# Differential attention units: GpSimd's product of the swapped rows with the sines is queued behind the last written addition of two softmax maps

## The chip, the core and the metric

The kernel runs on one core of one Trainium2 chip. The metric is the device time of one execution in microseconds (us); the time of a version is the median of its runs. Before the change it is 900.85 us, with three runs from 900.46 to 900.96.

The core has TensorE (PE in the profile, with its weight loads as PEld), VectorE (DVE), ScalarE (ACT), GpSimd (POOL) and SyncE (SP, which here only issues DMAs). Each works through a queue of its own in the order in which the program was laid out; between engines there are semaphores.

## The reference

A hybrid decoder block on x of 1024 rows by 1024 channels, float32. What matters here is the branch of differential attention, four heads with two maps each:

```python
h = rms_norm(x, g_pre)
qa, ka, va, fa, za, qb, kb, vb, zb, gates = split(h @ w_in)

def apply_rope(x, cos, sin):
    x1, x2 = split(x, 2, axis=-1)
    return concat([x1 * cos - x2 * sin, x2 * cos + x1 * sin])

qd = apply_rope(heads(qb), cos, sin)      # (heads, 2 maps, seq, 64)
kd = apply_rope(heads(kb), cos, sin)
p  = softmax(causal(qd @ kd.T / 8))       # both maps
pd = p[map 0] - lam * p[map 1]
yb = rms_norm(pd @ vd, g_subln) * (1 - lam_init)
```

Beside it runs an attention with forget gates (eight heads, no rope), both branches are gated, projected, merged and projected again, normalized, and added to x. None of that is touched.

## The kernel before

**Stages.** First the input is normalized and transposed (hT) and the values are projected (`v_block`). Then come eight attention units, u = 0 to 7: units 0 to 3 are the four differential heads, units 4 to 7 each hold two heads of the forgetting attention. Then come gates, branch projections and the output projection, which the change doesn't touch. float32 products are made from a rounded high part and a low part, so each projection has three matmuls for each of 8 slices of the contraction.

**A unit.** `unit_attn` makes four groups of two rows of 128 queries each. For a differential unit `row(i)` (lines 582 to 597) makes one row: `s_row` forms the scores of map 0 and of map 1 on PE (lines 492 and 493, tile S), DVE takes them out of PSUM with the mask and finds the extreme (line 495), ACT takes the exponential and the sum (line 501), DVE the reciprocal of both sums (line 591, tile l). GpSimd scales map 1 with its reciprocal and minus lambda (line 592), ACT scales map 0 (line 594), and GpSimd adds the two maps (line 595, the addition of the title). Later PE transposes the sum (line 522, tile pt), ACT and DVE split it in high and low part (lines 525, 526), and PE multiplies with the values (line 546). The width of row i is (i + 1) times 128, so in the profile the addition of row i of a unit is known by its shape: 128x128 is row 0, 128x1024 is row 7.

**Work laid between.** While unit u is attended, the projections of unit u + 1 are laid between its groups as fill tasks, in the order k first half (k0), q first half (q0), k second half (k1), q second half (q1), each half 512 columns; then the z projections of ZFILL. The loop at lines 708 to 723 writes the two rows of a group, the transposes and products of the group before, and then as many tasks as the weight of the groups done so far allows. By that count units 1 and 2 have k0 written behind row 1, q0 behind row 3, k1 and q1 behind row 5; unit 3, whose neighbour has four tasks and not six, has k0 behind row 1, q0 behind row 3, k1 behind row 5 and q1 behind row 7. The tasks of unit 0 are written before any row.

**Rope.** In a differential task the projected half lies in PSUM (tiles pk, pq of the pool pj, 2 buffers). `rope` (lines 359 to 371) copies it with ACT (line 362, raw), swaps blocks of 32 partitions with four small DMAs from SP's queue (line 366, raw to sw), multiplies with the cosines on DVE (line 368, rot), multiplies sw with the sines on GpSimd (line 369, the product of the title), and adds on DVE (line 370). `stack` then splits the result into high and low part (lines 378 and 379, tiles hi and lo) and sends both with four DMAs (lines 381 and 382) into TA, TB or KA, KB, from which the scores of the next unit are made.

**Buffers.** The tag "sw" has 2 buffers and serves sw and hi in turn; "raw" has 4 and serves raw, rot, lo and the staged z (line 432, tile sz, copied from PSUM at line 433). Taken in order, a rope with its stack takes three of "raw" and two of "sw". A staged z of units 1 and 2 follows twelve tiles of the four ropes, so the first z takes the buffer that lo of k1 had.

**Order on the engines.** The order in which each engine gets its instructions isn't the order of writing. The whole program is traced first, and a planner with its own estimate of durations (`schedule_with_timeline_sim=True`) orders each engine's queue by what it takes to be ready. `tc.issue_after(ins)` adds one constraint to that: what is traced in its block on the engine of `ins` comes behind `ins` in that engine's queue. It adds no instruction and no wait for the end of `ins`.

Of the kernel before, what the change touches and what calls it, by code (L numbers as in the profile page):

```python
# [12 lines left out]
ALU = mybir.AluOpType  # L13
# [32 lines left out]
def f32(ap):  # L46
    return ap.bitcast(F32)
# [3 lines left out]
def tile_hybrid_block(  # L51
# [18 lines left out]
    nc = tc.nc  # L70
# [54 lines left out]
    with ExitStack() as st:  # L125
# [152 lines left out]
        cosT, sinT, dmask = (big.tile([P, S], F32, tag="big", name=n) for n in ("cosT", "sinT", "dmask"))  # L278
# [27 lines left out]
                h_combinations(k)  # L306


    held = [None, None]

    def load_w(name, src, hi_act=False, lo_pool=False, pieces=None, behind=(None, None)):
        raw = wpool.tile([P, KT, P], F32, tag="wraw", name=f"raw_{name}")
# [17 lines left out]
    def project(ps, wt, c, ks=range(KT)):  # L330
        hi, lo = wt
        for k in ks:
            for a, h in ((hi, 0), (hi, 1), (lo, 0)):
                mm = nc.tensor.matmul(  # L334
                    ps, lhsT=a[:, k, :], rhs=hT[h][k // 4][c][:, k % 4, :],
                    start=(k == 0 and a is hi and h == 0), stop=(k == KT - 1 and a is lo))
        return mm.ins


    with ExitStack() as st:  # L340
# [9 lines left out]
        def unit_proj(u):  # L350

            diff = u < 4
            t = u if diff else u - 4
            qc, kc = (QB, KB_) if diff else (QA, KA_)
            T = {}
            for n in ("TA", "TB", "KA", "KB"):
                T[n] = qk.tile([P, S], F32R, tag=n, name=f"{n}{u}")

            def rope(ps, c, nm):
                sl = slice(c * CH, (c + 1) * CH)  # L360
                raw = stg.tile([P, CH], F32, tag="raw", name=f"raw{nm}", bufs=4)
                nc.scalar.copy(raw, ps)
                sw = stg.tile([P, CH], F32, tag="sw", name=f"sw{nm}")
                for b in range(4):
                    o = b ^ 1
                    nc.sync.dma_start(sw[b * 32:(b + 1) * 32, :], raw[o * 32:(o + 1) * 32, :])  # L366
                rot = stg.tile([P, CH], F32, tag="raw", name=f"rot{nm}", bufs=4)
                nc.vector.tensor_tensor(rot, ps, cosT[:, sl], op=ALU.mult)  # L368
                nc.gpsimd.tensor_tensor(sw, sw, sinT[:, sl], op=ALU.mult)
                nc.vector.tensor_tensor(rot, rot, sw, op=ALU.add)  # L370
                return rot

            def stack(A, B, src, sl, nm):

                if u > 0:
                    hi = stg.tile([P, CH], F32R, tag="sw", name=f"hi{nm}")
                    lo = stg.tile([P, CH], F32R, tag="raw", name=f"lo{nm}", bufs=4)
                    nc.scalar.copy(hi, src)
                    nc.vector.tensor_tensor(lo, src, hi, op=ALU.subtract)
                    for t, a, b in ((A, UPR, DNR), (B, DNR, UPR)):  # L380
                        nc.sync.dma_start(f32(t[a, sl]), f32(hi[a]))
                        nc.sync.dma_start(f32(t[b, sl]), f32(lo[a]))
                    return
                nc.scalar.copy(A[UPR, sl], src[UPR])
                nc.vector.tensor_tensor(A[DNR, sl], src[UPR], A[UPR, sl], op=ALU.subtract)
                nc.scalar.copy(B[DNR, sl], src[DNR])
                nc.vector.tensor_tensor(B[UPR, sl], src[DNR], B[DNR, sl], op=ALU.subtract)

            def q_chunk(wt, c):
                sl = slice(c * CH, (c + 1) * CH)  # L390
                ps = pj.tile([P, CH], F32, tag="pj", name=f"pq{u}_{c}")
                project(ps, wt, c)
                src = rope(ps, c, f"q{u}_{c}") if diff else ps
                stack(T["TA"], T["TB"], src, sl, f"q{u}_{c}")

            def k_chunk(wt, c):
                sl = slice(c * CH, (c + 1) * CH)
                ps = pj.tile([P, CH], F32, tag="pj", name=f"pk{u}_{c}")
                project(ps, wt, c)
                src = rope(ps, c, f"k{u}_{c}") if diff else ps  # L400
                stack(T["KA"], T["KB"], src, sl, f"k{u}_{c}")

            box = {}

            def mk(kind, c, c0):
                def run():
                    if kind not in box:
                        box[kind] = load_w(f"{kind}{u}", w_cols(c0))
                    (q_chunk if kind == "q" else k_chunk)(box[kind], c)
                return run  # L410

            tasks = [mk("k", 0, kc + t * P), mk("q", 0, qc + t * P),
                     mk("k", 1, kc + t * P), mk("q", 1, qc + t * P)]
            return T, tasks
# [146 lines left out]
        def unit_attn(u, T):  # L561
# [19 lines left out]
            if diff:  # L581
                def row(i, rows):
                    boff = S - (i + 1) * P
                    if "X" not in rows:
                        rows["X"] = [swapped(T, m, i // 2, f"d{u}") for m in range(2)]
                    le = small.tile([P, 2], F32, tag="l2", name=f"l{u}_{i}", bufs=4)
                    l1, l2 = le[:, 0:1], le[:, 1:2]
                    p1, _ = s_row(T, 0, i, rows["X"][0], dmask, boff, f"d{u}", l1)
                    p2, _ = s_row(T, 1, i, rows["X"][1], dmask, boff, f"d{u}", l2)
                    n = (i + 1) * P  # L590
                    nc.vector.reciprocal(le, le)
                    nc.gpsimd.tensor_scalar(
                        p2[:, 0:n], p2[:, 0:n], l2, nlam, op0=ALU.mult, op1=ALU.mult)
                    nc.scalar.activation(p1[:, 0:n], p1[:, 0:n], AF.Copy, scale=l1)
                    nc.gpsimd.tensor_tensor(
                        p1[:, 0:n], p1[:, 0:n], p2[:, 0:n], op=ALU.add)
                    rows[i] = p1

                def evac(g):
                    def run(yp):  # L600
                        ys = stg.tile([P, 2 * P], F32, tag="ys", name=f"ys{u}_{g}")
                        nc.scalar.copy(ys, yp)
                        nc.sync.dma_start(y_d[u][:, g * 2 * P:(g + 1) * 2 * P], ys)
                    return run

                for g in GORD[u]:
                    rows = {}
                    groups.append((
                        4 * g + 3,
                        [lambda i=i, rows=rows: row(i, rows) for i in (2 * g, 2 * g + 1)],  # L610
                        lambda g=g, rows=rows: av(rows, g, vt, 0, False, evac(g), f"d{u}_{g}", False)))
            else:
                ysb = {}

                def row(m, i, rows):
                    n = (i + 1) * P
                    diag = cb[m][:, n - P:n]
                    nc.gpsimd.tensor_tensor(diag, diag, trim, op=ALU.add)  # L618
                    if "X" not in rows:
                        rows["X"] = swapped(T, m, i // 2, f"f{u}")  # L620
                    p1, l1 = s_row(T, m, i, rows["X"], cb[m], 0, f"f{u}")
                    nc.vector.reciprocal(l1, l1)  # L622
                    held[1] = nc.gpsimd.tensor_scalar(  # L623
                        p1[:, 0:n], p1[:, 0:n], l1, 1.0, op0=ALU.mult, op1=ALU.mult).ins
                    rows[i] = p1

                def evac(m, g):
                    def run(yp):
                        if m == 0:
                            ysb[g] = stg.tile([P, 2 * P], F32, tag="ys", name=f"ys{u}_{g}")  # L630
                        tmp = stg.tile([P, 2 * P], F32, tag="yt", name=f"yt{u}_{m}_{g}", bufs=1)
                        nc.scalar.copy(tmp[64:128], yp[64:128])
                        nc.vector.tensor_tensor(
                            ysb[g][64 * m:64 * m + 64], yp[0:64], tmp[64:128], op=ALU.add)
                        if m == 1:
                            nc.sync.dma_start(y_d[u][:, g * 2 * P:(g + 1) * 2 * P], ysb[g])
                    return run

                for g in GORD[u]:
                    for m in range(2):  # L640
                        rows = {}
                        groups.append((
                            4 * g + 3,
                            [lambda m=m, i=i, rows=rows: row(m, i, rows) for i in (2 * g + 1, 2 * g)],
                            lambda m=m, g=g, rows=rows: av(
                                rows, g, vt, m * P, True, evac(m, g), f"f{u}_{m}_{g}",
                                u == 7 and g in FING)))
# [586 lines left out]
```

## Time and profile before

| | |
|---|---|
| median of 3 runs | 900.85 us (900.46 to 900.96) |
| the profiled execution's own time | 900.05 us |
| its span in the profile | 898.2 us |
| busy DVE, ACT, POOL over the span | 580.8, 429.5, 408.8 us |
| granted TensorE clock, mean | 0.998 |
| sine products (line 369) on POOL | 16, the median 1.29 us (four of them unit 0's) |
| additions of two maps (line 595) on POOL | 32, the median 1.43 us |

The times in the views run from the start of the span. The differential units lie at about 143 to 340 us, and the twelve sine products of units 1 to 3 between 144 and 282 us. In a timeline each row is one instruction or a few alike: start, duration, engine, line, operation, tile written and tiles read, shapes, the count, and in brackets the idle time of the engine just before with the event that ended it. A row of the waits names who waited for whom, with the total, the count and the longest. A row of the view by windows gives for each engine the busy time in that stretch.

### The profile page before, as it was taken

To read this page: it belongs to the slowest core of one execution; us is meant where nothing else is said; L and a number is where in the kernel's file an instruction comes from. 1 tells how busy PE (TensorE), PEld (TensorE's weight loads), DVE (VectorE), ACT (ScalarE), POOL (GpSimd) and SP (SyncE) were. 2 spreads that over 40 slices of the span, in tenths; PEclk is the share of its full clock that TensorE was granted. 3 is DMA by queue.
4 is the path that set the end of the run, shared out by engine and by line. 5 is a ranking of instruction groups with operands and counts; after the bars stand their busy time and mean duration, and the time that the engine had idled before them with its cause. 6 is when DMAs were issued, how large, how long until landed. Compare 5 with 4: busy or idle time off the path is not lost.

```text
span 898.2 us, 13825 instructions
## 1 busy us (share of the span) xinstructions
PE 882.4 (98%) x4612; PEld 746.5 (83%) x4612; DVE 580.8 (65%) x1124; ACT 429.5 (48%) x865; POOL 408.8 (46%) x400
## 2 busy tenths in 40 slices
PE   8999999999999999999999999999999999999997
PEld 6999987788888888888888888888888888888885
DVE  6766555868567644556547556626766896648797
ACT  7432225565766663464645646724443362314352
POOL 2234225636647544253444435516534323483963
PEclk9999999999999999999999999999999999999999
DMA  8576656656657754635636430397766598210495
GB/s 306 188 260 246 209 166 162 170 139 172 156 135 194 179 168 91 176 104 125 191 90 174 127 103 25 92 410 236 234 207 203 191 357 296 80 39 1 122 198 172
DMA packets 138186, 154.81 MB, mean 172 GB/s; under 512 B 12145, under 2 KB 98161, under 8 KB 137090
## 3 DMA queue, kind: packets, MB, share of 16 engines
q1 hardware_dynamic: 133744, 151.55, 55.8%
q0 software_dynamic: 4224, 2.10, 2.0%
q8 instruction: 37, 0.61, 0.3%
q14 instruction: 35, 0.29, 0.1%
q10 hardware_dynamic: 146, 0.27, 0.1%
HBM read 86.17 MB, written 38.34 MB: 139 GB/s over the span
## 4 chain that ended last, share of the span: by engine, by line
PE 75%; DMA 6%; DVE 5%; ACT 4%; SPq 4%; POOL 3%; issue 2%; POOLq 0%; DVEq 0%; ACTq 0%
PE x_g L831 15%; PE pb L991 10%; PE pv L214 10%; PE x_o L831 8%; PE pz L334 7%; PE pq L334 5%; PE pk L334 5%; PE ypf L546 3%; PE ptf L522 3%; SPq L366 2%; PE Sf L492 2%; PE Sf L493 2%; DMA swk<-rawk 1%; PE pg L334 1%; PE pgl L334 1%
## 5 line engine op out<-in xcount | busy, mean ns | idle before, releaser
L214 PE MATMUL pv<-wvhi,hT 128*128 128x264 f32 (+2 forms) x384 | 88.0, 323 | 0.3 <-ACT wvhi L160 0.3
L334 PE MATMUL pq<-hT,hi_q 128*128 128x512 f32 x256 | 82.1, 395 | 0.0
L334 PE MATMUL pz<-hT,hi_z 128*128 128x512 f32 x256 | 81.6, 394 | 0.4 <-DVE rotq L368 0.3
L334 PE MATMUL pk<-hT,hi_k 128*128 128x512 f32 x256 | 81.7, 393 | 0.0
L991 PE MATMUL pb<-yT,hi_br 128*128 128x512 f32 x256 | 78.7, 389 | 0.0
L831 PE MATMUL x_g<-T,a_g 128*128 128x512 f32 x336 | 78.0, 391 | 0.0
L831 PE MATMUL x_o<-wo_op,a_o 128*128 128x512 f32 x324 | 74.8, 392 | 0.0
L831 PEld LDWEIGHTS x_g<-T,a_g 128*128 128x128 f32 x336 | 63.1, 188 | 13.8
L831 PEld LDWEIGHTS x_o<-wo_op,a_o 128*128 128x128 f32 x324 | 60.7, 188 | 13.9 <-DVE a_o L768 0.5
L214 PEld LDWEIGHTS pv<-wvhi,hT 128*128 128x128 f32 x384 | 64.2, 190 | 6.2 <-ACT wvhi L160 0.6
L526 DVE TENSOR_TENSOR plf<-ptf,phf 128x512 fp32r<-128x512 f32 (+1 forms) x80 | 50.1, 635 | 25.8 <-ACT phf L525 25.1
L501 ACT ACTIVATE Pd<-Pd,mxd 128x128 f32<-128x128 f32 (+7 forms) x64 | 49.7, 777 | 32.5 <-DVE mxd L495 32.4
L618 POOL TENSOR_TENSOR cb<-cb,trim 128x128 f32<-128x128 f32 x64 | 29.4, 464 | 72.9 <-DVE mxf L495 50.8
L214 PE MATMUL pv<-wvlo,hT 128*128 128x256 f32 (+2 forms) x192 | 61.7, 326 | 0.0
L501 ACT ACTIVATE Pf<-Pf,mxf 128x1024 f32<-128x1024 f32 (+3 forms) x64 | 49.7, 777 | 24.9 <-DVE mxf L495 22.9
L831 PE MATMUL x_g<-hT,a_g 128*128 128x512 f32 x252 | 59.1, 392 | 0.0
L623 POOL TENSOR_SCALAR Pf<-Pf,lf 128x1024 f32<-128x1024 f32 (+3 forms) x64 | 47.9, 754 | 20.8 <-DVE lf L622 18.6
L525 ACT CAST phf<-ptf 128x512 fp32r<-128x512 f32 (+1 forms) x80 | 42.6, 543 | 30.8 <-PE ptf L522 26.5
L991 PEld LDWEIGHTS pb<-yT,hi_br 128*128 128x128 f32 x256 | 48.1, 188 | 9.9
L831 PEld LDWEIGHTS x_g<-hT,a_g 128*128 128x128 f32 x252 | 47.3, 188 | 10.4
L334 PEld LDWEIGHTS pz<-hT,hi_z 128*128 128x128 f32 x256 | 47.3, 188 | 9.6 <-DVE rotq L368 0.7
L334 PEld LDWEIGHTS pq<-hT,hi_q 128*128 128x128 f32 x256 | 47.2, 188 | 9.0
(277 smaller groups left out, 2289.8 us busy)
## 6 DMA issues: line engine op xcount, KB each, us to landing
t_d<-t SPq DMA_DIRECT2D x16, 512.0 KB, 4.1
T<-t_d SPq DMA_DIRECT2D x8, 1024.0 KB, 8.1
raw<-in_w_in_dram SPq DMA_DIRECT2D x14, 512.0 KB, 4.7
vb_d<-vbs SPq DMA_DIRECT2D x8, 512.0 KB
va_d<-vas SPq DMA_DIRECT2D x8, 512.0 KB, 3.9
raw_k<-in_w_in_dram SPq DMA_DIRECT2D x8, 512.0 KB, 4.3
raw_q<-in_w_in_dram SPq DMA_DIRECT2D x8, 512.0 KB, 4.5
V<-vb_d SPq DMA_DIRECT2D x4, 1024.0 KB, 6.1
```

The costliest lines, as they stand in the source:

```text
L214: nc.tensor.matmul(ps[n], lhsT=hT[hp][k // 4][i // 4][:, k % 4, hs], rhs=wt[k][:, a:b], start=first, stop=(k == KT - 1 and hp == 1))
L334: mm = nc.tensor.matmul(ps, lhsT=a[:, k, :], rhs=hT[h][k // 4][c][:, k % 4, :], start=(k == 0 and a is hi and h == 0), stop=(k == KT - 1 a ...
L366: nc.sync.dma_start(sw[b * 32:(b + 1) * 32, :], raw[o * 32:(o + 1) * 32, :])
L501: held[0] = nc.scalar.activation(pr[:, 0:n], pr[:, 0:n], AF.Exp, bias=mx[:, len(pcs) - 1:len(pcs)], scale=-1.0, accum_out=le).ins
L522: lasts[0] = nc.tensor.transpose(pt[:, o * P:(o + 1) * P], rows[2 * g + r][:, j * P:(j + 1) * P], ident).ins
L525: nc.scalar.copy(ph[:, 0:n], pt[:, 0:n])
L526: nc.vector.tensor_tensor(pl[:, 0:n], pt[:, 0:n], ph[:, 0:n], op=ALU.subtract)
L546: lasts[0] = nc.tensor.matmul(o, lhsT=a, rhs=b[:, src], start=(j == 0 and n == 0), stop=(odd == 1 and jj == g and n == len(prods) - 1)).ins
L618: nc.gpsimd.tensor_tensor(diag, diag, trim, op=ALU.add)
L623: held[1] = nc.gpsimd.tensor_scalar(p1[:, 0:n], p1[:, 0:n], l1, 1.0, op0=ALU.mult, op1=ALU.mult).ins
L831: nc.tensor.matmul(x[m], lhsT=a[:, ai, k, :], rhs=right[m][bi][k], start=(k == 0 and n == 0), stop=(k == 3 and n == 2))
L991: nc.tensor.matmul(ps, lhsT=a[:, kk, :], rhs=yT[g][h][:, k % 2, sl], start=(k == 0 and a is hi and h == 0), stop=(k == 3 and a is lo))
```

## The change

`row` keeps the instruction of its last traced addition in `lastp`; in `rope` the sine product is traced in a block that queues it on GpSimd behind that addition. Before the first row is written (unit 0's ropes) there is none, and nothing is held.

```diff
-    held = [None, None]
+    held, lastp = [None, None], [None]
...
                 nc.vector.tensor_tensor(rot, ps, cosT[:, sl], op=ALU.mult)
-                nc.gpsimd.tensor_tensor(sw, sw, sinT[:, sl], op=ALU.mult)
+                with tc.issue_after(lastp[0]) if lastp[0] else ExitStack():
+                    nc.gpsimd.tensor_tensor(sw, sw, sinT[:, sl], op=ALU.mult)
                 nc.vector.tensor_tensor(rot, rot, sw, op=ALU.add)
...
-                    nc.gpsimd.tensor_tensor(
-                        p1[:, 0:n], p1[:, 0:n], p2[:, 0:n], op=ALU.add)
+                    lastp[0] = nc.gpsimd.tensor_tensor(
+                        p1[:, 0:n], p1[:, 0:n], p2[:, 0:n], op=ALU.add).ins
```

No instruction is added or removed, no shape and no buffer changes.

## The prediction

> **What bounds the kernel now.** I read the busy line of the page first, then the view by windows over the stretch of the differential units, then the waits in it, then the timelines of GpSimd and of PE.
>
> ```profile
> PE 882.4 (98%) x4612; PEld 746.5 (83%) x4612; DVE 580.8 (65%) x1124; ACT 429.5 (48%) x865; POOL 408.8 (46%) x400
> ```
>
> ```profile
> 143.00:190.00 47.00, 45.23 (x233) 36.59 (x232) 32.57 (x81) 29.43 (x59) 29.70 (x24) 1.00 0.67 170
> 190.00:240.00 50.00, 49.97 (x278) 42.91 (x276) 36.37 (x89) 31.71 (x70) 27.70 (x23) 1.00 0.63 159
> 240.00:290.00 50.00, 49.77 (x282) 42.90 (x281) 33.46 (x84) 30.51 (x67) 28.69 (x26) 1.00 0.61 156
> ...
> 345.00:620.00 275.00, 271.30 (x1536) 233.21 (x1535) 154.19 (x397) 141.87 (x306) 113.50 (x155) 1.00 0.51 151
> ```
>
> PE is the bound: 882.4 of 898.2 us. In the three stretches where sine products of units 1 to 3 stand it is idle for 47.00 - 45.23 = 1.77 us, 0.03 and 0.23 us, 2.03 us in all; in the stretch behind, 3.70 us. That is what reordering can give. GpSimd is busy 29.70, 27.70 and 28.69 us there, some 58 in 100: what matters on it is the order, not the sum.
>
> ```profile
> DVE rotq L370 <- POOL swq L369: 14.6, 7, 4.2
> DVE rotk L370 <- POOL swk L369: 14.1, 8, 5.3
> ...
> PE ptd L522 <- POOL Pd L595: 1.1, 2, 0.9
> ```
>
> DVE sits at the head of its queue for 28.7 us waiting for products, and PE waits twice, 1.1 us in all, for an addition. So the addition reaches the bound, by little; a wait for the product does so only through DVE.
>
> **The change, part by part.** The `with` costs nothing by itself: no instruction is added, GpSimd works in order anyway. What counts is which of the twelve products change place. By the order of writing, units 1 and 2 hold k0 behind the addition of row 1 (128x256), q0 behind row 3 (128x512), k1 and q1 behind row 5 (128x768); unit 3 the same but q1 behind row 7 (128x1024). In GpSimd's timeline four stand behind theirs already, unit 3's k0 and q0 and these two, the q1 of units 1 and 2:
>
> ```profile
> 176.49 1.30 POOL L369 TENSOR_TENSOR swq<-swq,sinT 128x512 f32<-128x512 f32 x1
> ...
> 227.04 1.29 POOL L369 TENSOR_TENSOR swq<-swq,sinT 128x512 f32<-128x512 f32 x1 [0.45 <-DMA swq<-rawq]
> ```
>
> (They follow the 768-wide additions at 168.72 and 224.74, shown next.) The other eight are passed by their addition; each pair is product, then addition:
>
> ```profile
> 144.24 1.29 POOL L369 TENSOR_TENSOR swk<-swk,sinT 128x512 f32<-128x512 f32 x1 [0.33 <-DMA swk<-rawk]
> ...
> 146.57 1.14 POOL L595 TENSOR_TENSOR Pd<-Pd,Pd 128x128 f32<-128x128 f32 x2
> ...
> 153.52 1.91 POOL L369 TENSOR_TENSOR swq<-swq,sinT 128x512 f32<-128x512 f32 x1 [0.50 <-DMA swq<-rawq]
> ...
> 156.81 1.27 POOL L595 TENSOR_TENSOR Pd<-Pd,Pd 128x512 f32<-128x512 f32 x1
> ...
> 165.02 1.29 POOL L369 TENSOR_TENSOR swk<-swk,sinT 128x512 f32<-128x512 f32 x1 [0.27 <-DMA swk<-rawk]
> ...
> 168.72 1.84 POOL L595 TENSOR_TENSOR Pd<-Pd,Pd 128x768 f32<-128x768 f32 x1 [0.52 <-ACT Pd L594]
> ...
> 192.99 1.46 POOL L369 TENSOR_TENSOR swk<-swk,sinT 128x512 f32<-128x512 f32 x1 [5.17 <-DMA swk<-rawk]
> ...
> 200.02 0.74 POOL L595 TENSOR_TENSOR Pd<-Pd,Pd 128x256 f32<-128x256 f32 x1
> ...
> 203.46 1.30 POOL L369 TENSOR_TENSOR swq<-swq,sinT 128x512 f32<-128x512 f32 x1 [2.71 <-DMA swq<-rawq]
> ...
> 211.37 1.30 POOL L595 TENSOR_TENSOR Pd<-Pd,Pd 128x512 f32<-128x512 f32 x1
> ...
> 212.87 1.29 POOL L369 TENSOR_TENSOR swk<-swk,sinT 128x512 f32<-128x512 f32 x1 [0.20 <-DMA swk<-rawk]
> ...
> 224.74 1.85 POOL L595 TENSOR_TENSOR Pd<-Pd,Pd 128x768 f32<-128x768 f32 x1
> ...
> 268.95 1.30 POOL L369 TENSOR_TENSOR swk<-swk,sinT 128x512 f32<-128x512 f32 x1
> ...
> 270.20 1.83 POOL L595 TENSOR_TENSOR Pd<-Pd,Pd 128x768 f32<-128x768 f32 x1
> ...
> 280.45 1.30 POOL L369 TENSOR_TENSOR swq<-swq,sinT 128x512 f32<-128x512 f32 x1 [0.85 <-DMA swq<-rawq]
> ...
> 286.15 2.39 POOL L595 TENSOR_TENSOR Pd<-Pd,Pd 128x1024 f32<-128x1024 f32 x1
> ```
>
> If nothing else moved, a product would start where its addition ends: 147.71 for 144.24 (3.5 us later), 158.08 for 153.52 (4.6), 170.56 for 165.02 (5.5), 200.76 for 192.99 (7.8), 212.67 for 203.46 (9.2), 226.59 for 212.87 (13.7), 272.03 for 268.95 (3.1), 288.54 for 280.45 (8.1). Where the addition stood right behind the product it moves up by the product's 1.3 to 1.9 us, and the delay shrinks by as much. So the change **gives**: additions that start up to 1.9 us earlier; and **takes**: eight ropes whose last step, store and buffers come 2 to 14 us later.
>
> **The gain.** On PE these rows touch it:
>
> ```profile
> 158.13 0.77 PE L522 MATMUL ptd<-ident,Pd 128*128 128x128 f32 x5 [0.90 <-POOL Pd L595]
> 159.16 0.38 PE L492 MATMUL Sd<-KA,TA 128*128 128x256 f32 x1 [0.26 <-DVE mxd L495]
> ...
> 169.82 0.73 PE L334 MATMUL pz<-hT,hi_z 128*128 128x512 f32 x2 [0.33 <-DVE rotq L368]
> ```
>
> At 158.13 five transposes wait 0.90 us for the addition of row 3 (ended 158.08), which stood behind a product of 1.91 us: with the product out of the way that wait goes whole. At 159.16 scores wait 0.26 us for DVE, which before had waited for that product in line 370; at 169.82 a projection waits 0.33 us for DVE's cosine product, queued behind the rope that waited for the product of 165.02. I take all three, 0.90 + 0.26 + 0.33 = 1.49 us. At the bottom it is 0 (DVE may be late for another reason: then the same scores wait for loq), at the top the whole 2.03 us.
>
> **The loss.** What hides a late product is that the tiles made from it are used only by the next unit's fourth row and later. That cover is thin at three places, which I price from both sides:
>
> ```profile
> 180.69 0.73 PE L334 MATMUL pk<-hT,hi_k 128*128 128x512 f32 x2
> ...
> 232.14 0.62 PE L334 MATMUL pk<-hT,hi_k 128*128 128x512 f32 x2
> ...
> 290.81 0.62 PE L334 MATMUL pk<-hT,hi_k 128*128 128x512 f32 x2
> ```
>
> ```profile
> 230.67 0.57 ACT L433 COPY sz<-pz 128x512 f32<-128x512 f32 x1
> ...
> 283.08 0.58 ACT L378 CAST hik<-pk 128x512 fp32r<-128x512 f32 x1
> ```
>
> ```profile
> 171.11 2.45 SPq L366 DMA_DIRECT2D swq<-rawq  x4
> ```
>
> ```profile
> 162.21 2.65 DMA swk<-rawk
> ```
>
> (PE's timeline, ACT's, that of SP's queue, and the chain of work that ended last, where a row is a start, a duration and what ran.)
>
> *At 180.69* PE begins the next unit's k0, into the PSUM buffer that the first staged z empties. Product 165.02 at 170.56 frees its sw buffer (line 370) at 170.56 + 1.29 + 0.69 = 172.5; four stores and four loads on SP's queue, some 0.61 us each as the four loads of 171.11, and 2.65 us to land put the next product at 180.0, not 176.49: 3.5 us late, and so would be the z copies, which stood behind its rope on ACT. Ends: 0 if the planner puts the z copy ahead, 3.5 us if not.
>
> *At 232.14* the same of unit 2: the product at 226.59 ends 227.9, line 370 and both parts (0.69 us each, as the row of 281.78 below) take it to 230.0, four stores of 0.61 and 2.65 us to land to 235.1; lo's "raw" buffer is the one that the z copy of 230.67 takes. The copy ends at 235.7 and k0 starts 3.5 us late. Ends 0 and 3.5 us.
>
> *At 290.81* unit 4's k1 needs the PSUM buffer that hik (283.08) helps to empty, and hik takes the sw buffer that unit 3's last product leaves: 288.54 + 1.30 + 0.69 (line 370), two copies of 0.58 and 0.69 for the low part = 292.4, 1.6 us late. Ends 0 and 1.6 us (0 if the addition of row 7 comes up by 2.5 us, as its start waits for the reciprocal that DVE had behind line 370).
>
> The planner orders all queues anew with these delays in its own reckoning, and DVE can't stay as it is: the reciprocal of row 7 stood behind the rope that now follows row 7's addition. So I take the value of the nearest row, what a rope cost PE when it was late before, 0.33 us at 169.82, three times: 0.99 us. Ends 0 and 3.5 + 3.5 + 1.6 = 8.6 us.
>
> One row bears on a cost that GpSimd and DVE lay on each other:
>
> ```profile
> 270.28 2.31 DVE L370 TENSOR_TENSOR rotk<-rotk,swk 128x512 f32<-128x512 f32 x1 [1.80 <-POOL swk L369]
> ...
> 281.78 0.69 DVE L370 TENSOR_TENSOR rotq<-rotq,swq 128x512 f32<-128x512 f32 x1 [1.02 <-POOL swq L369]
> ```
>
> Line 370 takes 0.69 us alone, and 2.31 beside the addition of 270.20 to 272.03: it ended 0.56 us behind it. With that addition ahead of the product, line 370 has it no longer beside it. [...]
>
> **Sum.** -1.49 + 0.99 = -0.5 us on the span of 898.2: 897.7. The profiled execution took 900.05, 1.85 us around its span, and lies 0.80 under the median of the runs: 897.7 + 1.85 + 0.80 = 900.35, say **900.4 us**, 0.05% under 900.85. A measurement of this kernel can tell some 0.2% (1.8 us) from no change.
>
> **Rivals.** *Faster.* GpSimd's order gets right for the whole stretch, DVE's 28.7 us of waits shrink because the swapped rows have long landed when the product's turn comes, and the scores run ahead: the 2.03 us go whole, and of the 3.70 us behind a quarter, 0.92: -2.95, **897.9 us**. For it: each moved product stood at the head of GpSimd with an addition of the attention behind it. Against: from 190 to 290 us PE lost 0.26 us, so there is next to nothing to win with seven of the twelve products.
>
> *Slower.* The second k half of a unit comes so late that its buffers hold up z and the next unit's first projection: 3.5 us at 232.14 and half of the 3.5 at 180.69, where the ends differ only by ACT's order, less the gain of 1.49: +3.8, **904.7 us**. It decides from where unit 2's k1 product starts later than 226.59 - 3.5 = 223.1 us, and row 5's addition started at 224.74 there. For it: the serial course of load, product, addition, store and next load uses most of a unit: unit 2's four products reach from 192.99 to 227.04 us. Against: the planner sees the delay and can put scores and transposes, or other copies, ahead.
>
> *Not what it says.* The planner lays the rest so that additions and products merely trade places and every wait finds a new name: 900.85 us, within the forecast's case.
>
> **How the numbers follow.** Small sum or no effect: 0.44, of this 0.06 for the last rival; its own range is 900.85 ± 1.8, 899.05 to 902.65. Faster: 0.26; slower: 0.30, a little more, since the losses have the higher ends (8.6 against 2.03). A planner's new order further on, in units 4 to 7, can add to either. The range takes the points of both rivals and a little of their further ends: 897.6 to 905.0.
>
> **What would show it.** Right: on GpSimd all twelve products follow their additions; PE's wait of 0.90 us at 158 is gone; PE idle from 143 to 190 us falls from 1.77 to under 1 us; GpSimd's idle time ahead of products that a load ended, and DVE's waits in line 370, shrink. Loss terms: PE waiting at a k projection for a z copy near 180 and 232, for line 379 near 291, or for scores' operands of unit 3's row 4 near 299. The prediction is wrong if PE's idle time from 143 to 345 changes by more than 1.8 us, or if the difference lies behind 345, where no product stands.

## The result, and the profile after

The changed kernel takes 911.23 us (median of 5 runs, 909.52 to 913.13) against 900.85 for the kernel before (5 runs, 899.56 to 901.86). The ratio is 1.0116 with a 95% interval of 1.0100 to 1.0131: slower by some 10 us, above the 905.0 at which the predicted range ended. The profiled execution took 909.52 us with a span of 907.6, 9.4 longer than the one of before. The change adds a line, so line numbers from 370 on are one higher in the rows of the changed kernel (the sine product is 370, the rope's addition 371, hi and lo 379 and 380, the z copy 434, the addition of two maps 596).

First the busy line of its page, then its view by windows (in each: PE, PEld, DVE, ACT and POOL busy with their instructions, the granted clock, DMA share, GB/s).

```profile
PE 885.6 (98%) x4612; PEld 748.4 (82%) x4612; DVE 581.7 (64%) x1124; ACT 430.8 (47%) x865; POOL 407.6 (45%) x400
```

```profile
143.00:190.00 47.00, 41.72 (x213) 33.55 (x211) 35.74 (x82) 28.94 (x61) 28.75 (x24) 0.96 0.59 143
190.00:240.00 50.00, 48.86 (x259) 41.47 (x260) 33.45 (x80) 29.19 (x61) 21.84 (x19) 1.00 0.59 146
240.00:290.00 50.00, 48.94 (x266) 41.80 (x265) 31.64 (x78) 27.48 (x59) 29.13 (x23) 1.00 0.57 143
290.00:345.00 55.00, 53.69 (x299) 45.42 (x298) 29.83 (x85) 34.22 (x72) 25.76 (x25) 1.00 0.75 200
...
```

PE is busy 3.2 us longer for the same 4612 matmuls (885.6 against 882.4), its mean granted clock is 0.996 against 0.998, and it is idle for longer. From 143 to 345 us it stands idle for 5.28 + 1.14 + 1.06 + 1.31 = 8.79 us, where it was 1.77 + 0.03 + 0.23 + 0.10 = 2.13 before. These 6.7 us and 1.6 us at a slower clock (last section) are most of the 9.4; over half of the idle time is in the first stretch, where unit 1's halves are projected.

Its waits show for what PE stood (who waited for whom, total, times, longest).

```profile
PE Sd L493 <- DVE mxd L496: 3.7, 4, 1.2
...
PE ypd L547 <- ACT phd L526: 2.0, 3, 1.5
...
PE ptd L523 <- POOL Pd L596: 0.7, 1, 0.7
PE pk L334 <- ACT sz L434: 0.6, 1, 0.6
PE pk L334 <- DVE lok L380: 0.5, 1, 0.5
```

All of these but the last two are waits of the attention for its own steps. The z copy, with which the slower rival reckoned, ends a wait of 0.6 us at unit 3's k0 (245.07), and a low part of unit 4 ends one of 0.5 us at unit 4's k1 (302.01). So the waits name neither the sine product nor the rope of units 1 to 3; to see where these stand, one follows a half through the engines. These rows are from the timeline of all engines of the changed kernel, at unit 1's k1 and q1 (a start, a duration and what ran; in brackets the idle time just before).

```profile
169.98 1.85 POOL L596 TENSOR_TENSOR Pd<-Pd,Pd 128x768 f32<-128x768 f32 x1
171.77 1.30 POOL L370 TENSOR_TENSOR swk<-swk,sinT 128x512 f32<-128x512 f32 x1
173.11 0.69 DVE L371 TENSOR_TENSOR rotk<-rotk,swk 128x512 f32<-128x512 f32 x1 [0.83 <-POOL swk L370]
...
174.46 0.63 ACT L379 CAST hik<-rotk 128x512 fp32r<-128x512 f32 x1
...
176.31 0.57 ACT L362 COPY rawq<-pq 128x512 f32<-128x512 f32 x1
...
178.91 0.68 DVE L368 TENSOR_TENSOR rotq<-pq,cosT 128x512 f32<-128x512 f32 x1
...
179.64 1.22 PE L334 MATMUL pz<-hT,hi_z 128*128 128x512 f32 x2
```

The product follows its addition, as the change wants. But behind the held half stands the *next* one: q1's projection had left PE before 160 us, and its copy out of PSUM (line 362) runs on ACT at 176.31, behind hi of k1. With line 368 behind it, q1's PSUM buffer is free at 179.6, and in that moment the second half of z starts on PE. It started at 169.82 before: 9.8 us earlier. The same order stands in ACT's timeline of the kernel before, with hardly any time between:

```profile
167.11 0.62 ACT L378 CAST hik<-rotk 128x512 fp32r<-128x512 f32 x1 [0.36 <-ACT Pd L501]
...
168.48 0.56 ACT L362 COPY rawq<-pq 128x512 f32<-128x512 f32 x1
```

The reason, by this reading, is the shared tag: raw, rot and lo take turns in the four buffers of tag "raw" in the order of writing, and a half's raw copy is next in turn behind lo of the half before. The buffer that it gets needn't be the late one (counted in turn, q1's copy gets that of q0's lo); what holds the copy is its place in ACT's queue, behind hi of the half before. That the tag makes this order is tested below. A held product thus holds a PSUM buffer of the next half, and through it the projection two further on.

What PE lacks then is best seen with windows restricted to line 334, the projections, first after, then before.

```profile
168.00:179.60 11.60, 0.19 (x1) 0.00 (x0) 0.99 0.52 124
```

```profile
168.00:179.60 11.60, 6.49 (x25) 4.54 (x25) 1.00 0.57 137
```

In these 11.6 us the kernel before has 6.49 us of projections to put between the steps of the attention, the changed one next to none. All work on PE there, in the same window without that restriction, was 11.27 us before and is 9.16 now: without fill PE runs at the pace of the softmax. The lateness stays: unit 2's k0 starts at 191.84 (180.69 before), unit 3's at 245.07 (232.14).

### The profile page after: what moved, and what is told of

It reads as the page before. It is cut to its first block, busy times and chain, and to the rows that moved or that the text cites. A ratio compares the mean times of both kernels' runs of the same rounds, so it can differ in the third digit from the quotient of the medians.

```text
span 907.6 us, 13821 instructions
## 1 busy us (share of the span) xinstructions
PE 885.6 (98%) x4612; PEld 748.4 (82%) x4612; DVE 581.7 (64%) x1124; ACT 430.8 (47%) x865; POOL 407.6 (45%) x400
## 4 chain that ended last, share of the span: by engine, by line
PE 81%; DVE 5%; DMA 4%; issue 3%; ACT 3%; POOL 2%; SPq 1%; POOLq 0%; DVEq 0%; ACTq 0%
PE x_g L832 15%; PE pb L992 10%; PE pv L214 9%; PE x_o L832 8%; PE pz L334 8%; PE pk L334 7%; PE pq L334 6%; PE ypf L547 4%; PE ptf L523 3%; PE Sf L493 2%; PE Sf L494 2%; PE ypd L547 2%; PE pg L334 1%; PE pgl L334 1%; DVE Pd L496 1%
## 5 line engine op out<-in xcount | busy, mean ns | idle before, releaser
L593 POOL TENSOR_SCALAR Pd<-Pd,l,nlam 128x128 f32<-128x128 f32 (+7 forms) x32 | 30.9, 967 | 65.0 <-DVE l L592 53.4
```

Source lines behind the costliest of these rows:

```text
L593: nc.gpsimd.tensor_scalar(p2[:, 0:n], p2[:, 0:n], l2, nlam, op0=ALU.mult, op1=ALU.mult)
```

## The experiments

The expectations speak of theories by letter. Theory A: the loss is this chain, from a held product through the buffers to the next half's copy out of PSUM and to PE's projections. Theory B, the rival: the loss comes from elsewhere, from what the holds do to the attention or from the new order in which the planner lays everything. Three more letters part the same question otherwise. Theory C: the loss lies in the order that the planner gives PE under the hold. Theory D: the held rope itself keeps operands and PSUM from PE, whatever PE's order. Theory E: the late rope reaches PE by other ways than the copy out of PSUM. What each gives in numbers stands in each expectation. Each kernel is compared with runs of the kernel before on its own chip.

| kernel | median, us | ratio to before, 95% interval |
|---|---|---|
| only_k11 | 912.35 | 1.0108 to 1.0150 |
| not_k11 | 913.41 | 1.0118 to 1.0158 |
| before_rc | 905.38 | 1.0028 to 1.0066 |
| after_rc | 916.06 | 1.0148 to 1.0199 |
| hold_pe_old | 916.74 | 1.0155 to 1.0193 |
| free_pe_new | 913.51 | 1.0116 to 1.0171 |
| only_q10 | 909.23 | 1.0075 to 1.0119 |
| only_k31 | 902.95 | 0.9999 to 1.0041 |
| free_own | 909.70 | 1.0084 to 1.0124 |
| hold_own | 902.07 | 1.0009 to 1.0029 |
| hold_own_plan | 909.46 | 1.0079 to 1.0131 |
| free_own_plan | 907.59 | 1.0064 to 1.0112 |

**One hold, or all but that one.** only_k11 holds unit 1's k1 alone, the product whose chain is shown above; not_k11 holds the other eleven.

```diff
-                with tc.issue_after(lastp[0]) if lastp[0] else ExitStack():
+                with tc.issue_after(lastp[0]) if lastp[0] and nm == "k1_1" else ExitStack():
```

(`!=` in the second.)

> Only unit 1's second k half is held (behind row 5's addition); the other eleven products are free. Theory A (the held product holds up ACT's copy of the next half out of PSUM, since that copy takes its buffer behind the held half's low part; the PSUM buffer comes free late, the second z projection starts late, and PE runs out of work near 179 us): most of the 10.4 us, 906 to 910 us. Theory B (each held product costs about alike, by DVE waiting in line 371 and by a new order): an eighth of it, 902 us.

> All are held but unit 1's second k half. Theory A: the copy of unit 1's last half is free again, the second z projection starts near 170 us, 901 to 905 us. Theory B: seven eighths of the loss stay, 909 to 911 us.

Each alone costs as much as all twelve, so the losses don't add up and neither theory has its number. In only_k11 the second z comes at 178.01 and unit 2's k0 at 188.57, late as in the changed kernel. But PE also stands idle for 3.03 us between 240 and 290, where nothing is held. In not_k11 the second z comes at 175.31, not near 170, and the idle time is spread over all stretches. A single hold makes the planner lay all that follows anew; kernels that differ in a hold can't be compared by their sum alone.

**The smallest holds.** only_q10 holds unit 1's q0 alone, whose addition is the one for which PE waited 0.90 us; only_k31 holds unit 3's k1 alone, which moves by the least. The edit is as above, with "q0_1" and "k1_3".

> Only unit 1's first q half is held, behind row 3's addition: the place of the 0.90 us wait at 158 us on which the forecast's gain rests. If the step of the gain is right and nothing else moves: 899.3 to 900.5 us. Theory C: the planner rewrites the order from there on, 904 to 912 us. Theory D: the next copy out of PSUM comes some 3 us late, 901 to 904 us.

> Only unit 3's second k half is held; its addition came right behind it before, so the product is 2 to 3 us later, the smallest hold of the eight. Theory D: at most 902 us. Theory C, if the planner's order is upset by any hold: 904 us or more.

In only_q10 the wait of 0.90 us is gone (one of 0.84 us for another addition now stands at 170.07), but the kernel is slower by 8.9 us, with 3.07 and 2.34 us of PE idle in the two stretches from 190 to 290, behind the place of the hold: the gain is lost in the new order. That is theory C's outcome, and D's 901 to 904 us was missed. only_k31 can't be told from no change; its 902.95 lies between D's bound and C's and decides nothing.

**Raw copies apart.** before_rc and after_rc give the raw copies two buffers of their own ("rc") and rot and lo two; the cosine product reads the raw copy, so that ACT's copy alone frees PSUM. z's halves are staged one in each tag. The first holds nothing, the second holds all.

```diff
-                raw = stg.tile([P, CH], F32, tag="raw", name=f"raw{nm}", bufs=4)
+                raw = stg.tile([P, CH], F32, tag="rc", name=f"raw{nm}", bufs=2)
...
-                rot = stg.tile([P, CH], F32, tag="raw", name=f"rot{nm}", bufs=4)
-                nc.vector.tensor_tensor(rot, ps, cosT[:, sl], op=ALU.mult)
+                rot = stg.tile([P, CH], F32, tag="raw", name=f"rot{nm}", bufs=2)
+                nc.vector.tensor_tensor(rot, raw, cosT[:, sl], op=ALU.mult)
...
-                    zs = stg.tile([P, CH], F32, tag="raw", name=f"s{nm}_{c}", bufs=4)
+                    zs = stg.tile([P, CH], F32, tag=("raw", "rc")[c], name=f"s{nm}_{c}", bufs=2)
```

> The kernel before, with buffers of their own for the copies out of PSUM (two, and two for rot and lo), and the cosine product made from the copy and not from PSUM, so that PSUM comes free with the copy alone. The base for the next run. Both theories: within 4 us of 900.9.

> The changed kernel with the same buffers as the base ahead. Theory A: the hold no longer reaches PSUM, so at most 3 us over that base. Theory B: 8 to 12 us over that base, as DVE still waits for each held product.

The hold costs 10.7 us here too (916.06 against 905.38), theory B's 8 to 12. The base lies 4.5 us above 900.9, a little more than was expected. The two projections named above are on time, 164.38 and 180.48 us. But the first z is staged in the tag of rot and lo. One of the two z copies comes only at 190.27: ACT stood idle for 2.34 us in front of it, for the low part of the held q1, and PE waits for that copy. These rows are from the timelines of ACT and of PE in after_rc:

```profile
190.27 0.58 ACT L434 COPY sz<-pz 128x512 f32<-128x512 f32 x1 [2.34 <-DVE loq L380]
...
191.00 0.71 PE L334 MATMUL pq<-hT,hi_q 128*128 128x512 f32 x2 [3.58 <-ACT sz L434]
```

So the edit moved the chain from one copy out of PSUM to another. As a test of A it failed; as a reading it says that any copy out of PSUM that stands behind a late low part will do.

**Order and hold taken apart.** In hold_pe_old all twelve are held, and each instruction of PE's queue is tied behind the one that precedes it in the kernel before, without any wait between them; the other engines are planned. free_pe_new holds nothing, and PE's queue is tied to the order of the changed kernel.

```diff
+        for a, b in zip(order, order[1:]):
+            tc.add_manual_dep(traced[b], traced[a].name, NoSync)
```

> All twelve products are held as in the change, but PE's queue is pinned, instruction by instruction, to the order that it had before; the planner orders the other engines. Theory C (the loss lies in the order that the planner gives PE under the hold: attention first, projections late): 899 to 904 us. Theory D (the held rope itself keeps operands and PSUM from PE, whatever PE's order): 908 to 916 us, with PE waiting at the places where the old order wants the late tiles.

> Nothing is held, but PE's queue is pinned to the order that it got with the change. Theory C: 907 to 912 us, as with the change. Theory D: 899 to 903 us.

With PE's order kept, the loss is larger, against theory C and 0.7 us above D's range, and its waits have one name. Here the waits of hold_pe_old from 140 to 345 us, and one of them followed through the timeline of all engines, at unit 2:

```profile
PE pz L334 <- DVE rotq L368: 10.1, 2, 5.4
...
PE pq L334 <- DVE rotq L368: 2.9, 2, 2.1
...
PE pz L334 <- DVE rotk L368: 1.5, 1, 1.5
```

```profile
231.87 1.81 POOL L596 TENSOR_TENSOR Pd<-Pd,Pd 128x768 f32<-128x768 f32 x1
...
233.63 1.26 POOL L370 TENSOR_TENSOR swk<-swk,sinT 128x512 f32<-128x512 f32 x1
...
234.93 0.69 DVE L371 TENSOR_TENSOR rotk<-rotk,swk 128x512 f32<-128x512 f32 x1 [1.85 <-POOL swk L370]
...
235.66 0.62 ACT L379 CAST hik<-rotk 128x512 fp32r<-128x512 f32 x1 [3.98 <-DVE rotk L371]
...
236.18 0.58 ACT L362 COPY rawq<-pq 128x512 f32<-128x512 f32 x1
...
236.92 0.68 DVE L368 TENSOR_TENSOR rotq<-pq,cosT 128x512 f32<-128x512 f32 x1
...
237.66 1.22 PE L334 MATMUL pz<-hT,hi_z 128*128 128x512 f32 x2 [5.42 <-DVE rotq L368]
```

From the addition to PE every step follows the one above it. The projection that the copy empties had ended by 223.6 us, and ACT was idle for 3.98 us in front of hi: as far as the profile shows, only the copy's place in ACT's queue held it. PE loses 5.42 us at this place and 10.1 + 2.9 + 1.5 = 14.5 us in all, for the copy of the next half out of PSUM and for nothing else of size. That is theory A's chain in the open.

free_pe_new has no hold and costs 13 us all the same, against theory D and 1.5 us above C's range. So the order that PE got with the change is slow by itself: its waits in 140 to 345 us are again those of the attention, and one for the forget gates (tile ft).

```profile
PE ft L676 <- DVE fs L667: 4.1, 1, 4.1
PE Sd L492 <- DVE mxd L495: 3.0, 5, 1.0
PE ptd L522 <- POOL Pd L595: 2.2, 3, 1.8
...
```

**The chain taken away.** hold_own holds all twelve, ties PE to the order of before, and cuts the chain: raw copies and both staged halves of z have a tag of their own with three buffers, rot and lo have two, the X tiles of the scores two instead of three (for the room), and the cosine product reads the raw copy. free_own is the same with nothing held.

```diff
-                raw = stg.tile([P, CH], F32, tag="raw", name=f"raw{nm}", bufs=4)
+                raw = stg.tile([P, CH], F32, tag="rc", name=f"raw{nm}", bufs=3)
...
-                    zs = stg.tile([P, CH], F32, tag="raw", name=f"s{nm}_{c}", bufs=4)
+                    zs = stg.tile([P, CH], F32, tag="rc", name=f"s{nm}_{c}", bufs=3)
...
-            t = qk.tile([P, 2 * P], F32R, tag=f"X{m}", name=f"X{m}{nm}_{g}", bufs=3)
+            t = qk.tile([P, 2 * P], F32R, tag=f"X{m}", name=f"X{m}{nm}_{g}", bufs=2)
```

> The base for the next run: nothing held, PE's queue pinned to the order of before; copies out of PSUM and staged z's have three buffers of their own, the swapped operands X two and not three, and the cosine product reads the copy, so PSUM comes free with the copy alone. All theories: 900 to 906 us.

> All twelve products held, PE's queue pinned as in hold_pe_old, with the buffers of the base ahead. Theory A (a held product holds up the next half's copy out of PSUM and its cosine product, and PE's next projection waits for them, 14.5 us in hold_pe_old): these waits go, and it comes within 4 us of free_own. Theory E (the late rope reaches PE by another way too, its stored operands or DVE waiting in line 371): 8 us or more over free_own, with PE waiting for DMAs, for line 496 or for transposes.

hold_own takes 902.07 us, within 0.3% of the kernel before and 14.7 below hold_pe_old, close to the 14.5 us of waits that it was to remove. All that is left of PE's waits from 140 to 345 us:

```profile
PE Sd L493 <- DVE mxd L496: 2.0, 2, 1.9
PE Sd L494 <- DMA X0d<-TA: 0.8, 1, 0.8
PE ypd L547 <- DVE pld L527: 0.2, 1, 0.2
```

There is none for a copy out of PSUM. ACT's timeline of hold_own shows why: q1's copy now runs ahead of hi of k1.

```profile
159.14 0.56 ACT L362 COPY rawq<-pq 128x512 f32<-128x512 f32 x1
...
171.47 0.62 ACT L379 CAST hik<-rotk 128x512 fp32r<-128x512 f32 x1 [1.27 <-DVE rotk L371]
```

That it is the tag shows in all kernels. Units 1 to 3 have nine copies with a half of the same unit before them (q0, k1 and q1 of each). In the eight kernels where raw, rot and lo share one tag, the copy comes behind hi of the half before in all 72 cases, held or not. In the six where the copies are apart it comes ahead in 41 of 54, among them 34 of the 36 in units 1 and 2.

Theory E is out: hold_own isn't slower than its base, and the waits for line 496 and for a DMA come to 2.8 us. But free_own, the base, missed its expectation: 909.70 us, 7.6 more than with the hold, so that A's "within 4 us of free_own" was missed too. Part of the 7.6 shows in free_own's timeline:

```profile
178.47 2.09 POOL L595 TENSOR_TENSOR Pd<-Pd,Pd 128x896 f32<-128x896 f32 x1
178.94 2.17 DVE L379 TENSOR_TENSOR loq<-rotq,hiq 128x512 fp32r<-128x512 f32 x1
181.04 0.68 DVE L495 CUSTOM_DVE_ANT_0 Pd<-Sd,dmask 128x512 f32<-128x512 f32 x1
...
181.78 0.47 PE L492 MATMUL Sd<-KB,TB 128*128 128x128 f32 x1 [2.26 <-DVE mxd L495]
```

An unheld rope's low part (line 379) runs beside an addition, takes 2.17 us, and line 495 and PE's scores stand behind it for 2.26. The rest of the 7.6 us isn't settled, so they aren't counted as a gain of the hold.

**The same buffers, all planned.** The last pair leaves PE's queue to the planner as well.

> All twelve products held, with the buffers of hold_own (raw copies and staged z in a tag of their own with three buffers, rot and low parts with two, X tiles with two, cosine product from the raw copy), but every queue ordered by the planner, PE's too. Theory A (only the copy out of PSUM behind the held half costs): with that tie gone the planner has no reason to put the projections late, unit 2's k0 starts near 181 us and not 191.8, and the time is that of hold_own, 902 us, to 904. Theory B (the hold makes the planner choose a slow order whatever the buffers, which free_pe_new and the scattered waits of the softmax speak for): 907 to 913 us, with waits of PE for line 496 and the additions.

> The same buffers with nothing held and every queue ordered by the planner: the base of hold_own_plan. Theory A: 902 to 906 us, as before_rc (905.4), and hold_own_plan within 3 us of it. Theory B: hold_own_plan at least 5 us slower than this. If this one is as slow as free_own (909.7), then the smaller buffers and the cosine product from the raw copy, and not PE's pinned order, made free_own slow.

The two differ by 1.9 us, and their intervals overlap: with the chain gone the hold costs little in the planner's own order too, which was A's condition, and theory B's difference of at least 5 us isn't there. Unit 2's k0 starts at 173.68 us in hold_own_plan, where it was 191.84 in the changed kernel: the projections are no longer late. A's absolute numbers were missed, 902 to 904 with the hold and 902 to 906 without, and 909.46 lies in B's 907 to 913. The base is slow by itself: 907.59 with nothing held and PE's order planned, 909.70 with that order tied. So most of what makes these bases slow came with the buffers and the cosine product, not with PE's tied order. Taken together, the price of the hold over its own base:

| buffers; order of PE's queue | nothing held | twelve held | difference |
|---|---|---|---|
| as before; planned | 900.85 | 911.23 | +10.4 |
| as before; that of before | 900.34 | 916.74 | +16.4 |
| raw copies apart, z behind lo; planned | 905.38 | 916.06 | +10.7 |
| raw copies and z apart; planned | 907.59 | 909.46 | +1.9 |
| raw copies and z apart; that of before | 909.70 | 902.07 | -7.6 |

(In the second row the base is the kernel before, as it ran beside hold_pe_old.) While a copy out of PSUM stands behind a held half, the hold costs 10 us and more; where none does, 2 us or less. No version here beats the kernel before.

## Why the prediction was wrong

**The step that failed** is the loss, summed to 0.99 us. It fails in its first sentence: "What hides a late product is that the tiles made from it are used only by the next unit's fourth row and later." The tiles made from it, yes; their buffers are used much sooner. The next half's raw copy takes its buffer behind lo of the held half, so each held product holds PSUM, and PE's next projections but one. The prediction saw this kind of chain only at a unit's end, between lo of k1 and the z copy, and priced three places at "0.33 us at 169.82, three times: 0.99 us". The chain stands behind the held halves, not at the unit's end alone, and with PE's order kept it is worth 14.5 us. At the priced places the changed kernel has waits of 0.6 us (the z copy, unit 3's k0) and 0.5 us (unit 4's k1), together about the 0.99; the rest of the 6.7 us of idle time lies where no price was put.

**The row that showed it was read with the wrong sign.** The projection that waits 0.33 us for line 368 at 169.82 was counted as a gain, since the rope ahead of it had waited for a product. It was the end of this chain: the second half of z, waiting for q1's copy out of PSUM behind hi of k1. Holding k1's product pushes it further out, to 179.64.

**The gain** was of the right kind and too small to matter. PE's wait of 0.90 us at 158 is gone, as this row of the changed kernel's PE timeline shows, where the same five transposes start without one:

```profile
159.40 0.71 PE L523 MATMUL ptd<-ident,Pd 128*128 128x128 f32 x5
```

But PE's idle time from 143 to 190 didn't fall below 1 us, it rose to 5.28. The two smaller waits found other names. (The count beside it, seven of the twelve products between 190 and 290 us, should be eight; no sum rests on it.) **The places** were right: all twelve products start behind their additions, the eight that were to move among them (unit 2's k1 at 228.54 us for 212.87).

**The slower rival** had sign and kind: buffers that hold up z and the next unit's first projection. Its deciding point, k1's product of unit 2 later than 223.1, was passed by 5.4 us. Its price of 3.8 us was taken from the ends of units 1 and 2 (3.5 us and half of 3.5, less the gain of 1.49), where the loss was 10.4. **Its counter-argument**, that the planner can put scores and transposes ahead, came true and was no help: it did put them ahead, and PE then had no projections to lay between them. Unit 2's k0 came 11.15 us late, and the span ended 9.4 us late.

**Where it lies** was right: 6.7 us of idle time and the clock (below) before 345 us. The condition named as proof of error, idle time there up by over 1.8 us, is met.

**What stays open.** That the tag puts the copy behind hi is shown; that the planner chose the rest of its order because of it is argued, not shown. The order itself costs as much without a hold (free_pe_new), and planned orders with little or no hold cost 7 to 9 us too (only_q10, free_own_plan), so how much of the 10.4 us another order would have spared isn't known. Nor is it known which part of the edit (fewer buffers for rot, lo and X, or the cosine product from the copy) makes the bases of the last two pairs slow.

## What to carry to other kernels

Before an instruction is queued later, follow the buffers of everything behind it, not only its result: ask which copy out of PSUM takes its buffer in turn behind the late tile, and which projection waits for that PSUM. Here the projections laid between the steps of the attention were what kept PE busy (11.27 of 11.6 us with them, 9.16 with next to none), and the holds that delayed them cost PE time while its waits named mostly the attention's own steps. And where a planner lays all queues anew at each edit, tie the order of the engine that bounds before two versions are compared: a single held product moved this kernel by 12 us at one place and by nothing measurable at another. Tying it makes the waits name their cause; it doesn't make every difference clean, as free_own shows, which is tied like hold_own and 7.6 us slower without the hold.

## What was unexpected of the hardware

**The clock fell with no idle time of PE over 1.22 us near it.** The windows of the changed kernel have a granted clock of 0.66 from 178 to 183 us, with 1.00 on both sides:

```profile
168.00:178.00 10.00, 8.65 (x54) 6.91 (x52) 7.58 (x18) 8.29 (x16) 6.10 (x5) 1.00 0.55 132
178.00:183.00 5.00, 3.86 (x10) 2.98 (x11) 4.90 (x12) 3.59 (x6) 3.84 (x3) 0.66 0.49 107
183.00:190.00 7.00, 6.38 (x38) 4.84 (x37) 5.29 (x7) 3.29 (x8) 4.15 (x3) 1.00 0.06 19
```

PE's timeline there shows what it costs:

```profile
179.04 0.38 PE L493 MATMUL Sd<-KA,TA 128*128 128x256 f32 x1 [1.22 <-DVE mxd L496]
...
180.66 0.63 PE L334 MATMUL pz<-hT,lo_z 128*128 128x512 f32 x1
181.09 1.05 PE L334 MATMUL pz<-hT,hi_z 128*128 128x512 f32 x2
...
183.08 0.40 PE L334 MATMUL pz<-hT,lo_z 128*128 128x512 f32 x1
183.31 0.62 PE L334 MATMUL pz<-hT,hi_z 128*128 128x512 f32 x2
```

From 180.66 to 181.09 a matmul of 512 columns takes 0.43 us, from 183.08 to 183.31 it takes 0.23. The eight matmuls of the projection between 179.64 and 183.08 take 3.44 us where eight of 0.23 would take 1.84: 1.6 us lost. The clock granted from 180 to 183 us is 0.52, which agrees with the 0.23 and 0.43 us. The longest idle time of PE from 168 to 190 us is the 1.22 us at 179.04; from 168 to 178 PE had been busy for 8.65 of ten microseconds, 39 of its 54 matmuls (transposes among them) with 256 columns or fewer. What made the clock fall stays open.

**The cosine product out of SBUF** took 2.50 us beside an addition on GpSimd, out of PSUM 0.68. This is from the timeline of hold_own:

```profile
173.19 2.11 POOL L596 TENSOR_TENSOR Pd<-Pd,Pd 128x896 f32<-128x896 f32 x1 [0.40 <-ACT Pd L595]
...
173.36 2.50 DVE L368 TENSOR_TENSOR rotq<-rawq,cosT 128x512 f32<-128x512 f32 x1
```

The one out of PSUM, at 178.91 us in the changed kernel (the row is in the first timeline above), ran beside an addition of 178.35 to 180.45. All 16 of that kernel take 0.68 to 0.69 us; the 11 of hold_own between 143 and 290 us take 0.69 to 2.50, with medians of 1.07 (six of q) and 0.97 (five of k). In hold_own the buffers that cut the chain so cost DVE time, which may be a part of why the bases with them are slow.
